# Half of a projection double chunk's closing sums added in device memory by accumulating DMAs

## The chip, the cores and the metric

The kernel runs on one core of a Trainium2 chip. The metric is the device time of one execution in microseconds (us); lower is better. Times before and after are medians of runs.

## The reference, cut to what matters

One layer works on 256 rows of 4096 channels, all in float32:

```
h    = layer_norm(x)                              # 256 x 4096
proj = h @ w_in                                   # 4096 x 24592
q_r,k_r,v_r,g_r, q_f,k_f,v_f,g_f, f, gate = split(proj)
y_r  = group_norm(retention(rotary(q_r), rotary(k_r), v_r)) * silu(g_r)
y_f  = forgetting_attention(q_f, k_f, v_f, f) * silu(g_f)
m    = sigmoid(gate0) * (y_r @ w_branch_ret) + sigmoid(gate1) * (y_f @ w_branch_fox)
out  = layer_norm(ALPHA * h + m @ w_out)
```

The first 16384 columns of `proj` (the eight operands of the two branches) are what the change touches. The kernel writes them to a device-memory scratch tensor, `proj_d`, and the branches read them back from there later.

## The kernel before, in words

A float32 product is made of three products of split operands: each operand is kept as a high part and a low part, and `three` (lines 198 to 200) multiplies high by high, high by low and low by high. The weights arrive as raw float32 in tiles `wraw` (three buffers, loaded by SP, line 137). `split_into` turns them into the two parts: ACT casts the high part (line 153) and the vector engine, DVE, subtracts it from the raw value (line 154).

The first part of the kernel makes the projection. After two gate chunks it works in double chunks of 1024 columns, 20 of them: four for gates and then 16 for the branches' operands. A double chunk goes over the 4096 input channels in 16 steps of 256 (`PAIRS`). In eight of these the 2 x 2 block product (two row tiles by two column halves) is made with eight block products, in the other eight (`SEVEN`) with seven, for which DVE forms sums of weight blocks (`ta`, `tb`, lines 184 to 187) and both engines split them (`tset`). TensorE, PE, so has 8 x 24 + 8 x 21 = 360 matmuls of 512 columns in a double chunk. They accumulate in all eight PSUM banks under the keys 1 to 7 and x: the plain steps add to 2, 3, 4 and x, which are the four output blocks, and the seven-product steps add to all but x.

At the end of a double chunk `proj_evac` has ACT copy the eight banks to SBUF tiles `ev` (line 397): two under the tag `bias`, six under `w1`. PE can't start the next double chunk's products in a bank before that copy. The closing sums are those of `combine` (line 402), a generator that `late_step` moves on by one piece after each step. For the branches' operands it runs eight DVE sums on `ev` tiles (line 416) and stores the four output blocks from GpSimd's queue (POOL, line 408, 256 KB each):

```
op("2", "2", "1", ALU.add)         # block (0,0) = 2 + 1
op("1", "6", "1", ALU.add)
op("5", "5", "1", ALU.add)
op("3", "3", "5", ALU.subtract)    # block (0,1) = 3 - (5 + 6 + 1)
op("1", "7", "1", ALU.add)
op("4", "4", "1", ALU.add)         # block (1,0) = 4 + (7 + 6 + 1)
op("5", "7", "5", ALU.add)
op("x", "x", "5", ALU.subtract)    # block (1,1) = x - (7 + 5 + 6 + 1)
```

The order on each engine isn't the order of the program: a planner simulates a timeline and issues what is ready there by priority, so the pieces of `combine` can stand close together behind the copies. A wait of an instruction holds up all that is queued behind it on its engine.

After the last double chunk the remaining gate chunks run, and beside them the generators `retention` and `forgetting`. These fetch their operands from `proj_d` on POOL's queue (line 466: `rab`, `v`, `gn`, `nat`). `silu` (line 476) takes the fetched `gn`. Then come the two branch projections and the output projection, which the change does not touch.

Of the kernel before, what the change touches and what calls it, by code (L numbers as in the profile page):

```python
# [10 lines left out]
AF = mybir.ActivationFunctionType  # L11
ALU = mybir.AluOpType

P = 128
# [9 lines left out]
NC = 512  # L24
# [11 lines left out]
def hybrid_kernel(  # L36
# [5 lines left out]
    nc = tc.nc  # L42
    x, b_gate, b_forget = aps["x"], aps["b_gate"], aps["b_forget"]
# [15 lines left out]
    proj_d = dram.tile([S, 4 * RW + 4 * FW], F32, name="proj_d")  # L59
# [4 lines left out]
    def bcast(ap1, n0, n):  # L64
        return ap1[n0:n0 + n].rearrange("(o n) -> o n", o=1).to_broadcast([P, n])
# [314 lines left out]
    late = []  # L380
# [8 lines left out]
    def proj_evac(c0, gate=False):  # L389
        def f(m):  # L390
            v = {}
            for i, k in enumerate("x1265374"):
                if i < 2:
                    v[k] = work.tile([P, NC], F32, name="ev", tag="bias", bufs=2)
                else:
                    v[k] = work.tile([P, NC], F32, name="ev", tag="w1", bufs=6)
                nc.scalar.copy(v[k], m[k])  # L397
            late.append(combine(c0, v, gate))
        return f

    def combine(c0, v, gate):


        def put(t, i, k):
            if gate:
                nc.scalar.activation(v[k], v[k], AF.Sigmoid)
            to = gates_d if gate else proj_d
            nc.gpsimd.dma_start(to[t * P:(t + 1) * P, c0 + i * NC:c0 + (i + 1) * NC], v[k])

        def shift(i):  # L410
            gb = work.tile([P, NC], F32, name="gshift", tag="gshift", bufs=1)
            nc.gpsimd.dma_start(gb, bcast(b_gate, c0 + i * NC, NC))
            return gb

        def op(o, x, y, how):
            nc.vector.tensor_tensor(v[o], v[x], v[y], op=how)

        yield
        if gate:
            gb = shift(0)  # L420
            yield
            yield
            nc.vector.tensor_tensor(v["1"], v["1"], gb, op=ALU.add)
            yield
            nc.vector.tensor_tensor(v["5"], v["5"], gb, op=ALU.subtract)
            gb = shift(1)
            yield
        op("2", "2", "1", ALU.add)
        put(0, 0, "2")
        yield  # L430
        op("1", "6", "1", ALU.add)
        yield
        if gate:
            nc.vector.tensor_tensor(v["5"], v["5"], gb, op=ALU.subtract)
            yield
        op("5", "5", "1", ALU.add)
        yield
        op("3", "3", "5", ALU.subtract)
        put(0, 1, "3")
        yield  # L440
        op("1", "7", "1", ALU.add)
        yield
        op("4", "4", "1", ALU.add)
        put(1, 0, "4")
        yield
        op("5", "7", "5", ALU.add)
        yield
        op("x", "x", "5", ALU.subtract)
        put(1, 1, "x")
# [435 lines left out]
    for i in range((GATE1 - GATE0) // 2):  # L885
        add_pair("w_in", hTh, hTl, sops, PAIRS, proj_evac(gates[GATE0 + 2 * i][0], True))
    for i in range(16):
        add_pair("w_in", hTh, hTl, sops, PAIRS, proj_evac(2 * i * NC))
# [239 lines left out]
```

## Time and profile before

| | before |
|---|---|
| median of 3 runs | 2848.55 us (2847.6 to 2850.07) |
| profiled execution | 2845.76 us |
| its span, first to last instruction | 2844.0 us |
| PE busy | 2793.1 us, 98% |
| DVE busy | 2305.3 us, 81% |
| ACT busy | 1565.1 us, 55% |
| POOL busy | 169.8 us, 6% |
| mean granted TensorE clock | 0.997 |

Busy time is the time in which an engine has an instruction in work; issuing DMAs does not count. A stall is the idle time just before an instruction, with the engine and line that released it. The profile counts its times from the span's start; the double chunks of the branches' operands run from about 453 to 1775 us.

### The profile page before, as it was taken

Reading aid. Unit: us, or ns where it says so; the run is one execution under the profiler, and the core shown is the slowest. Engines: PE = TensorE matmul, PEld = TensorE weight load, DVE = VectorE, ACT = ScalarE, POOL = GpSimd, SP = SyncE. Lnnn points to the kernel's source line nnn. Section 1 sums busy time; section 2 is a strip of 40 time slices with the busy share of each in tenths; the row PEclk is TensorE's granted clock in tenths of the full one; section 3 lists DMA queues with packets and bytes.
Section 4 is the critical chain, followed back from the end, with each engine's and each line's share of the span. In section 5 each row is a group of like instructions: output and inputs, shape, how many; then the busy total and the mean of one; then the engine's idle time right before and its main releaser. Section 6 shows DMA issues by size and latency. Waiting matters only on the chain. (4 is left out here: it accounts for less than half of the span.)

```text
span 2844.0 us, 34687 instructions
## 1 busy us (share of the span) xinstructions
PE 2793.1 (98%) x12666; PEld 2308.8 (81%) x12666; DVE 2305.3 (81%) x2988; ACT 1565.1 (55%) x2170; POOL 169.8 (6%) x302
## 2 busy tenths in 40 slices
PE   7999999999999999999999999999999999999998
PEld 5788888888887887888878888788898888888886
DVE  7899999998999988989889888877675656656666
ACT  5565666656555655555555565445664444444443
POOL 1000000000000000000000000212220000000000
PEclk9999999999999999999999999999999999999999
DMA  6556655665566655556656656866676566666564
GB/s 221 198 207 239 225 219 214 230 224 205 214 222 222 222 211 211 211 211 222 222 213 218 221 204 224 290 229 202 204 232 216 211 215 211 226 215 231 210 233 170
DMA packets 128156, 620.28 MB, mean 218 GB/s; under 512 B 15803, under 2 KB 16075, under 8 KB 87019
## 3 DMA queue, kind: packets, MB, share of 16 engines
q1 hardware_dynamic: 105552, 543.47, 52.8%
q0 software_dynamic: 21856, 72.49, 8.2%
q8 instruction: 99, 1.62, 0.2%
q10 hardware_dynamic: 576, 2.10, 0.2%
q14 instruction: 73, 0.60, 0.1%
HBM read 588.54 MB, written 29.46 MB: 217 GB/s over the span
## 5 line engine op out<-in xcount | busy, mean ns | idle before, releaser
L153 ACT CAST whi<-wraw 128x1024 fp32r<-128x1024 f32 (+1 forms) x640 | 586.3, 945 | 373.7 <-PE ps L200 262.1
L154 DVE TENSOR_TENSOR wpart<-wraw,wpart 128x512 fp32r<-128x512 f32 (+2 forms) x790 | 520.4, 667 | 314.0 <-ACT wpart L153 311.9
L153 ACT CAST wpart<-wraw 128x512 fp32r<-128x512 f32 (+2 forms) x790 | 475.3, 606 | 525.5 <-DVE wpart L154 314.4
L154 DVE TENSOR_TENSOR wlo<-wraw,whi 128x1024 fp32r<-128x1024 f32 (+1 forms) x640 | 680.8, 1084 | 8.7 <-ACT whi L153 7.2
L199 PE MATMUL ps<-wlo,hTh 128*128 128x512 f32 x960 | 373.7, 389 | 0.0
L200 PE MATMUL ps<-whi,hTl 128*128 128x512 f32 x960 | 373.4, 389 | 0.0
L198 PE MATMUL ps<-whi,hTh 128*128 128x512 f32 x960 | 340.2, 390 | 5.8 <-ACT ev L397 5.6
L184 DVE TENSOR_TENSOR ta<-wraw 128x1024 f32<-128x1024 f32 x160 | 195.6, 1222 | 137.6 <-DMA wraw<-in_w_in 136.5
L153 ACT CAST tset<-tb 128x1024 fp32r<-128x1024 f32 x160 | 169.3, 1058 | 183.8 <-DVE tb L187 183.6
L199 PE MATMUL acc<-wlo,hTh 128*128 128x512 f32 x640 | 249.1, 391 | 3.4 <-DVE wlo L154 3.4
L200 PE MATMUL acc<-whi,hTl 128*128 128x512 f32 x640 | 247.8, 389 | 0.0
L198 PE MATMUL acc<-whi,hTh 128*128 128x512 f32 x640 | 242.2, 389 | 0.4 <-ACT whi L153 0.4
L153 ACT CAST tset<-ta 128x1024 fp32r<-128x1024 f32 x160 | 167.6, 1048 | 120.1 <-DVE ta L184 119.8
L198 PEld LDWEIGHTS ps<-whi,hTh 128*128 128x128 f32 x960 | 180.2, 188 | 46.4 <-ACT ev L397 9.1
L199 PE MATMUL acc<-wpart,hTh 128*128 128x512 f32 (+2 forms) x568 | 212.2, 377 | 4.2 <-DVE wpart L154 4.1
L200 PEld LDWEIGHTS ps<-whi,hTl 128*128 128x128 f32 x960 | 180.2, 188 | 37.6
L199 PEld LDWEIGHTS ps<-wlo,hTh 128*128 128x128 f32 x960 | 180.2, 188 | 37.3
L200 PE MATMUL acc<-wpart,hTl 128*128 128x512 f32 (+2 forms) x568 | 208.2, 370 | 0.6 <-DVE rstd L96 0.6
L154 DVE TENSOR_TENSOR tset<-tb,tset 128x1024 fp32r<-128x1024 f32 x160 | 195.0, 1219 | 4.7 <-ACT tset L153 4.7
L154 DVE TENSOR_TENSOR tset<-ta,tset 128x1024 fp32r<-128x1024 f32 x160 | 194.8, 1217 | 0.4
L199 PE MATMUL acc<-wpart,mTh 128*128 128x512 f32 x500 | 194.6, 389 | 0.0
L200 PE MATMUL acc<-wpart,mTl 128*128 128x512 f32 x500 | 194.5, 389 | 0.0
(257 smaller groups left out, 4853.3 us busy)
## 6 DMA issues: line engine op xcount, KB each, us to landing
wraw<-in_w_in SPq DMA_DIRECT2D x320, 1024.0 KB, 4.9
wraw<-in_w_out SPq DMA_DIRECT2D x128, 512.0 KB, 4.1
wraw<-in_w_in SPq DMA_DIRECT2D x112, 512.0 KB, 4.8
wraw<-in_w_branch_ret SPq DMA_DIRECT2D x64, 512.0 KB, 4.2
wraw<-in_w_branch_fox SPq DMA_DIRECT2D x64, 512.0 KB, 4.2
proj_d<-ev POOLq DMA_DIRECT2D x64, 256.0 KB, 3.5
g<-gates_d POOLq DMA_DIRECT2D x16, 512.0 KB, 5.7
wraw<-in_w_in SPq DMA_DIRECT2D x16, 272.0 KB, 4.5
```

The source lines that it names most:

```text
L153: c = nc.scalar.copy(hi, src)
L154: nc.vector.tensor_tensor(lo, src, hi.bitcast(F32), op=ALU.subtract)
L184: nc.vector.tensor_tensor(ta, B[0][:, None, :].to_broadcast([P, 2, NC]), raw[:, NC:3 * NC].rearrange("p (a n) -> p a n", a=2), op=ALU.add)
L198: nc.tensor.matmul(o, lhsT=a[0], rhs=w[0], start=first, stop=False)
L199: nc.tensor.matmul(o, lhsT=a[0], rhs=w[1], start=False, stop=False)
L200: return nc.tensor.matmul(o, lhsT=a[1], rhs=w[0], start=False, stop=last)
```

## The change

The gate double chunks keep `combine`. For the other 16, `proj_evac` has ACT write the negative of bank 5, and a new generator, `gather`, stores the tiles 2, 3, 4 and x as they are, each to its output block in `proj_d`. DVE makes four sums on the other four tiles. Each result is then sent to one of the same blocks by a DMA that adds to what is there (`accum_op`). The accumulating DMA must wait until the plain store of its block has landed.

```diff
-                nc.scalar.copy(v[k], m[k])
-            late.append(combine(c0, v, gate))
+                if k == "5" and not gate:
+                    nc.scalar.activation(v[k], m[k], AF.Identity, scale=-1.0)
+                else:
+                    nc.scalar.copy(v[k], m[k])
+            late.append(combine(c0, v, True) if gate else gather(c0, v))
         return f
+
+    def gather(c0, v):
+
+
+        def put(t, i, k, how=None):
+            to = proj_d[t * P:(t + 1) * P, c0 + i * NC:c0 + (i + 1) * NC]
+            if how is None:
+                nc.gpsimd.dma_start(to, v[k])
+            else:
+                nc.gpsimd.dma_start(to, v[k], accum_op=how)
+
+        def op(o, x, y, how):
+            nc.vector.tensor_tensor(v[o], v[x], v[y], op=how)
+
+        yield
+        for t, i, k in ((0, 0, "2"), (0, 1, "3"), (1, 0, "4"), (1, 1, "x")):
+            put(t, i, k)
+            yield
+        put(0, 0, "1", ALU.add)
+        op("6", "6", "1", ALU.add)
+        yield
+        op("5", "5", "6", ALU.subtract)
+        put(0, 1, "5", ALU.add)
+        yield
+        op("6", "6", "7", ALU.add)
+        put(1, 0, "6", ALU.add)
+        yield
+        op("7", "5", "7", ALU.subtract)
+        put(1, 1, "7", ALU.add)
```

## Rows read from the trace of the kernel before

**Rows 1.** The page's first part: busy us (share), instructions.
```profile
PE 2793.1 (98%) x12666; PEld 2308.8 (81%) x12666; DVE 2305.3 (81%) x2988; ACT 1565.1 (55%) x2170; POOL 169.8 (6%) x302
```
**Rows 2.** PE's waits, 480 to 1800 us: waiter, releaser, total us, times, longest.
```profile
PE ps L198 <- ACT ev L397: 4.4, 6, 1.4
PE acc L199 <- DVE wlo L154: 3.4, 4, 1.0
PE acc L199 <- DVE wpart L154: 2.1, 1, 2.1
PE acc L198 <- ACT tset L153: 0.9, 2, 0.4
PE acc L198 <- ACT whi L153: 0.4, 1, 0.4
```
**Rows 3.** PE's timeline, rows with a stall: start, us, what, idle before.
```profile
1042.41 0.50 PE L199 MATMUL acc<-wlo,hTh 128*128 128x512 f32 x1 [1.00 <-DVE wlo L154]
...
1704.41 0.50 PE L199 MATMUL acc<-wlo,hTh 128*128 128x512 f32 x1 [0.41 <-DVE wlo L154]
1706.15 0.50 PE L199 MATMUL acc<-wlo,hTh 128*128 128x512 f32 x1 [1.00 <-DVE wlo L154]
```
**Rows 4.** DVE's timeline behind the double chunk's end at about 1030 us.
```profile
1029.85 0.68 DVE L416 TENSOR_TENSOR ev<-ev 128x512 f32<-128x512 f32 x1
...
1040.54 0.68 DVE L416 TENSOR_TENSOR ev<-ev 128x512 f32<-128x512 f32 x1
1041.14 1.22 DVE L154 TENSOR_TENSOR wlo<-wraw,whi 128x1024 fp32r<-128x1024 f32 x1
```
**Rows 5.** Groups by line and shape: busy us, mean ns of one, idle before.
```profile
L416 DVE TENSOR_TENSOR ev<-ev 128x512 f32<-128x512 f32 x160 | 106.7, 683 | 0.0
L397 ACT COPY ev<-ps 128x512 f32<-128x512 f32 x80 | 47.9, 620 | 0.0
L406 ACT ACTIVATE ev<-ev 128x512 f32<-128x512 f32 x16 | 10.3, 645 | 1.9 <-DVE ev L416 1.9
L634 ACT ACT_TABLE_LOAD x5 | 6.4, 1283 | 0.4 <-DVE nm L631 0.3
```
**Rows 6.** Windows: length, busy PE, PEld, DVE, ACT, POOL, clock, DMA share, GB/s.
```profile
1442.00:1470.00 28.00, 26.58 (x114) 20.85 (x113) 27.52 (x33) 18.20 (x24) 2.16 (x4) 1.00 0.63 230
1470.00:1524.00 54.00, 54.00 (x240) 44.71 (x239) 46.13 (x50) 30.02 (x32) 0.00 (x0) 1.00 0.57 206
1780.00:1800.00 20.00, 17.81 (x86) 14.28 (x85) 17.50 (x25) 9.24 (x15) 7.25 (x12) 1.00 0.99 367
```
**Rows 7.** DMA, 1442 to 1470 us: POOL's queue; issues, median us to landing.
```profile
q0 software_dynamic: 320, 1.05, 9.4%
wraw<-in_w_in SPq DMA_DIRECT2D x5, 1024.0 KB, 6.3
proj_d<-ev POOLq DMA_DIRECT2D x4, 256.0 KB, 3.7
```
**Rows 8.** The same view, 1470 to 1524 us.
```profile
wraw<-in_w_in SPq DMA_DIRECT2D x11, 1024.0 KB, 4.8
```
**Rows 9.** POOL's timeline where the branches begin.
```profile
1774.96 1.45 POOL L466 DMA_DIRECT2D rab<-proj_d  x2 [8.14 <-PE ps L200]
1776.91 0.57 POOL L408 DMA_DIRECT2D proj_d<-ev  x1 [0.49 <-DVE ev L416]
...
1783.05 0.73 POOL L466 DMA_DIRECT2D gn<-proj_d  x1
```
**Rows 10.** Line 408 alone: its DMAs' time to landing, all of the span.
```profile
DMA to landing us min/median/max: 2.3/3.7/8.8
```
**Rows 11.** ACT's timeline and PE's, just behind.
```profile
1791.56 1.06 ACT L476 ACTIVATE sg<-gn 128x1024 f32<-128x1024 f32 x1 [0.48 <-DMA gn<-proj_d]
1789.22 0.50 PE L199 MATMUL acc<-wpart,hTh 128*128 128x512 f32 x1 [2.10 <-DVE wpart L154]
```

## The prediction

> **What bounds the kernel now.** I read the page's busy times first [rows 1]: PE is busy 98% of the span, so whatever is done on another engine can only win back PE's idle time. The second view is the list of what PE waited for between 480 and 1800 us, the stage of the changed sums and the hand-over to the branches [rows 2]. The reader should see how short it is: 4.4 + 3.4 + 2.1 + 0.9 + 0.4 = 11.2 us in 1320. That is the ceiling for named gains, 0.39% of the time. The three kinds have different causes. Six stalls wait for ACT to empty a PSUM bank at a double chunk's end (4.4 us). Seven wait for a split weight on DVE or ACT (3.4 + 0.9 + 0.4 = 4.7 us). One, of 2.1 us, comes at 1789 us, where the branches begin.
>
> The third view is PE's timeline, which says where the seven lie: all follow a double chunk's end by 12 to 14 us, and only five of the 16 ends have any; the first and the last end's are shown [rows 3]. DVE's timeline there gives the reason [rows 4]: the eight closing sums stand from 1029.85 to 1040.54 between the splits, the late split starts at 1041.14, and PE starts at 1042.41. The windows say the same in shares [rows 6]: in the 28 us around an end DVE is busy 27.52 us, in the 54 us behind it 46.13. So DVE has slack in a double chunk but none around its end, and that is where the change acts.
>
> **What the change removes.** Four of eight sums go, in 16 double chunks: 64 sums. One shows as 683 ns [rows 5], but the next DVE instruction starts 0.60 us after it (1040.54 to 1041.14, rows 4), so an end loses 4 x 0.60 = 2.4 us of DVE's queue and the whole stage 38 us. Of these, only what PE waits for counts. At the worst end the two stalls make 0.41 + 1.00 = 1.41 us [rows 3]; no other of the seven is over 1.0 [rows 2]. All are shorter than 2.4, so with loads on time all 4.7 us go. The bounds are 0 (the planner puts other work in the freed slots) and -4.7.
>
> **What it adds on ACT.** The negated copy of bank 5 is an activation in place of a copy. The trace has no such instruction on a bank; the nearest row is the sigmoid of the same size, 645 ns against 620 for a copy [rows 5]. I take 25 ns longer: 16 x 0.025 = 0.4 us of ACT, with PE's bank 5 behind it at most, so nothing to 0.4 on the path. Bounds: a little less than a copy, or, were the tables to be loaded each time, 1.28 us [rows 5] x 16 = 20.5 us of ACT, half of which could reach PE. I take 0, since ACT is idle a third of the 28 us (18.20 busy, rows 6).
>
> **What it adds on the DMA engines.** Instead of four stores an end has eight DMAs of 256 KB, four of them accumulating. What a plain one takes follows from POOL's queue around an end [rows 7]: four take 9.4% of 28 us, 2.6 us or 0.66 us each of all 16 engines. No row shows an accumulating one. From below it is 0.66 us, since as many bytes leave SBUF; from above I take the whole 3.7 us that a plain store needs to land [rows 7], as if the engines were held all that time. The DMA engines are idle for 37% of the 28 us [rows 6], 10.4 us, so between 2.6 and 14.8 us are wanted where 10.4 are free. I take 0.66, the measured row nearest to it.
>
> Free on average is not free for each load. Weight loads take 6.3 us around an end [rows 7] and 4.8 behind it [rows 8]. I put the 1.5 us between down to the four stores, and let four more cost another 1.5. A load that comes later makes DVE later by as much, so of the 2.4 us won 0.9 are left. The two ends with one stall of 1.00 keep 0.1 each (3.4 less the 1.41 of the last end leaves 2.0 for two), the last keeps 0.5, the rest go: 4.7 - 0.7 = 4.0 us gained. That is the first term.
>
> **Queues and waits.** POOL issues the four stores as soon as ACT has copied 2, 3, 4 and x, and doesn't wait for DVE any more. Behind them the first accumulating DMA waits for its store to land, 3.7 us [rows 7], by which time ACT is just through its copies; the other three wait for DVE's sums. In the projection only other DMAs of `gather` are queued behind. The `ev` tiles are held until the last accumulating DMA has landed, two landings of 3.7 us and four sums behind the copies, and are wanted again only at the next end, some 82 us on (16 ends between 453 and 1775 us). SP's queue and the loads' order don't move.
>
> At the hand-over it is different. POOL's queue holds the branches' fetches among the last stores [rows 9], and the DMA engines are busy 99% from 1780 to 1800 us [rows 6]. There the DVE relief of 2.4 us covers the stall of 2.1 [rows 11], but 4 x 0.66 = 2.6 us more of DMA come out of a full machine: -2.1 + 2.6 = +0.5 us, the second term.
>
> **Sum.** -4.0 + 0.5 = -3.5 us. The profiled execution took 2845.76 us (span 2844.0 and 1.8 around it), which gives 2842.3; it is 2.8 us below the median of the runs, 2848.55, and on that scale I predict 2845.0.
>
> **Rivals.**
> *An accumulating DMA costs like two plain ones.* It has to fetch what lies in the block before it writes, so twice the bytes move. Then the four cost 5.3 us, the loads are not 1.5 but 3.0 us later, and this is 0.6 more than DVE wins. The five ends that already stall get 5 x 0.6 = 3.0 us worse, and the hand-over is -2.1 + 5.3 = +3.2. Together +6.2 if every delay reaches PE, some +3.5 if half the hand-over's and two thirds of the ends' do: 2852. For it: the bytes. Against: 10.4 us of idle DMA around an end, and 11 ends that have slack. The row shows 0.66 us for a plain store [rows 7]. The Trainium skill ("Collectives: The Full Stack", section "The bandwidth ceiling: the fold count and why AG ≠ RS ≠ AR") says that an add inside a DMA costs nothing itself but needs two source reads, and so gives half a copy's rate; by it the price would be an estimated 1.3 us and the time this rival's, by the row alone it is the forecast's. No run here has shown it yet.
>
> *POOL's queue is held at the hand-over.* If the planner puts the first accumulating DMA before the fetch of `gn`, that fetch waits until a store has landed. Issued at 1776.9 and landing in up to 8.8 us [rows 10], the store frees the queue at 1785.7, so `gn` goes 2.7 us later than at 1783.05 [rows 9]. ACT's sigmoid already waits for it, 0.48 us [rows 11], and the weight casts are queued behind. That is +2.7 on the forecast: 2847.7. Against: the planner may fetch first.
>
> *The banks' stalls go as well.* With less on DVE the splits that ACT does before its copies come earlier, and the 4.4 us [rows 2] fall too, with the hand-over's 2.1: -11.2, 2837.3. For: the copies wait in ACT's order behind casts. Against: those casts depend on work from before the closing sums, which the change doesn't touch.
>
> *Slower: the accumulating DMAs hold the engines.* At 3.7 us each, 14.8 us are wanted in a 28 us window with 10.4 free. The loads lose 4.4 us at every end, DVE has gained 2.4, so PE loses 2.0 x 16 = 32 us, and 14.8 - 2.1 = 12.7 at the hand-over: +45, 2893. It decides from (10.4 + 2.4) / 4 = 3.2 us each. For: nothing in the trace accumulates, so nothing rules it out. Against: three times what even doubled bytes would ask.
>
> **How the numbers follow.** Forecast 0.40; doubled cost 0.20; POOL held 0.10; banks too 0.15; engines held 0.15. A measurement can't tell under 0.2%, 5.7 us, from no change. Faster by more (below 2842.8) is the banks' case and a tenth of the forecast's and others' spread: 0.24. Slower by more (above 2854.3) is the held engines and a third of the doubled cost: 0.22. The same: 0.54. The range goes from the banks' case, 2838, to 2862, a held-engines case that is just past its deciding point; it leaves out most of that case and a little below.
>
> **What would show it.** Line 416 should have 96 sums in place of 160 and DVE some 40 us less busy time. The seven stalls 12 us behind an end should be nearly gone, the bank stalls stay near 4.4 us. Weight loads around an end should land in about 7.8 us, accumulating DMAs in no more than 5, and DMA share should be 0.72 instead of 0.63. At the hand-over PE's stall should stay near 2 to 3 us. I am wrong if an accumulating DMA takes well over 1.3 us of the engines, if PE stalls appear at ends that had none, or if the bank stalls change by more than 3 us.

## The result, and the profile after

The changed kernel takes 2890.34 us (median of 4 runs, 2886.89 to 2893.39) against 2848.07 for the one before on the same chip: 42 us more, ratio 1.0151 with a 95% interval of 1.0131 to 1.017. Slower was clear, and outside my range. The profiled execution took 2892.81 us, 47.1 more than that of before.

The page's first part and POOL's DMA queue of the changed kernel (busy us and share; packets, MB, share of 16 engines):

```profile
PE 2812.1 (97%) x12666; PEld 2311.9 (80%) x12666; DVE 2271.4 (79%) x2924; ACT 1561.2 (54%) x2170; POOL 227.9 (8%) x366
...
q0 software_dynamic: 31072, 89.27, 11.3%
```

DVE did lose its 64 sums (2988 to 2924 instructions) and 34 us of busy time [rows 1]. POOL's busy time does count its DMA issues: the 64 accumulating ones are nearly all of the 58 us that it gained. What PE waited for between 480 and 1800 us:

```profile
PE ps L198 <- ACT ev L400: 15.6, 8, 3.0
PE acc L198 <- ACT tset L153: 11.9, 12, 2.2
PE acc L199 <- DVE wlo L154: 5.7, 7, 1.1
PE acc L199 <- DVE tset L154: 2.4, 6, 0.4
PE acc L198 <- ACT whi L153: 0.9, 2, 0.7
```

The 11.2 us of [rows 2] have become 36.5. The wait for ACT's copies at an end, 4.4 before, is the largest, and 18 stalls in place of two wait for `tset`. These stalls don't show all: adding up by how much the starts of successive matmuls lie further apart than their usual 0.227 us, from 540 to 1770 us, PE lost 17 us before and 62 after. So the whole loss is in the projection.

A double chunk's end of the changed kernel and the calm stretch behind it, then 4 us of the first (columns as in [rows 6]):

```profile
1389.00:1417.00 28.00, 25.74 (x107) 20.97 (x106) 24.94 (x28) 18.25 (x24) 5.71 (x8) 0.94 0.82 261
1417.00:1471.00 54.00, 54.00 (x240) 44.72 (x240) 46.18 (x48) 29.91 (x32) 0.00 (x0) 1.00 0.58 209
1392.00:1396.00 4.00, 4.00 (x12) 3.11 (x12) 3.91 (x6) 4.00 (x8) 1.88 (x4) 0.57 0.71 199
```

Around this end the DMA engines are busy 82% of the time (63% before) and DVE 24.94 of 28 us (27.52 before): DVE has got its slack, and PE has lost more. The last row shows a side effect: behind a stall of 2.26 us the granted clock was 0.57 for 4 us, mostly the lower of TensorE's two levels (1.2 and 2.4 GHz). That came at three ends, 5 us in all.

The DMA view of those 28 us, to be read against [rows 7]:

```profile
q0 software_dynamic: 896, 2.10, 31.2%
...
wraw<-in_w_in SPq DMA_DIRECT2D x5, 1024.0 KB, 6.6
proj_d<-ev POOLq DMA_DIRECT2D x8, 256.0 KB, 6.0
```

POOL's DMAs take 31.2% of 28 us, 8.7 us, where the four plain stores took 2.6. Over 14 ends the mean is 8.9 us, so an accumulating DMA costs (8.9 - 2.6) / 4 = 1.57 us of all 16 engines against 0.66 for a plain one, 2.4 times. The Trainium skill ("Collectives: The Full Stack", section "The bandwidth ceiling: the fold count and why AG ≠ RS ≠ AR") has a collective's adding transfers at half a copy's rate because the add needs two source reads; the trace agrees in kind, at somewhat more than double, and doesn't show what is read.

POOL's timeline at the same end, and line 412 (the accumulating DMAs) by its own view and its group beside the negated copy (line 398) and the sums (line 415):

```profile
1391.74 0.57 POOL L410 DMA_DIRECT2D proj_d<-ev  x1 [69.02 <-ACT ev L400]
1392.72 0.56 POOL L410 DMA_DIRECT2D proj_d<-ev  x1 [0.40 <-ACT ev L400]
1394.69 0.54 POOL L410 DMA_DIRECT2D proj_d<-ev  x1 [1.41 <-ACT ev L400]
1395.54 0.88 POOL L412 DMA_DIRECT2D proj_d<-ev  x1 [0.31 <-DMA proj_d<-ev]
1397.55 0.56 POOL L410 DMA_DIRECT2D proj_d<-ev  x1 [1.13 <-ACT ev L400]
1400.54 1.75 POOL L412 DMA_DIRECT2D proj_d<-ev  x2 [2.43 <-DMA proj_d<-ev]
1405.11 0.85 POOL L412 DMA_DIRECT2D proj_d<-ev  x1 [2.82 <-DMA proj_d<-ev]
```
```profile
DMA to landing us min/median/max: 4.7/8.2/13.0
```
```profile
L412 POOL DMA_DIRECT2D proj_d<-ev x64 | 56.5, 938 | 107.3 <-DMA proj_d<-ev 90.4 <-DVE ta L184 8.2 <-DVE ev L415 3.6
L415 DVE TENSOR_TENSOR ev<-ev 128x512 f32<-128x512 f32 x64 | 44.0, 688 | 1.9
...
L398 ACT ACTIVATE ev<-acc 128x512 f32<-128x512 f32 x16 | 10.0, 622 | 0.0
```

All eight DMAs go out within 14 us of the end, and the accumulating ones take a median of 8.2 us to land.

### The profile page after: what moved, and what is told of

The parts are those of the page before. It is cut to its first block, busy times and chain, and to the rows that moved or that the text cites. A ratio compares the mean times of both kernels' runs of the same rounds, so it can differ in the third digit from the quotient of the medians.

```text
span 2891.0 us, 34731 instructions
## 1 busy us (share of the span) xinstructions
PE 2812.1 (97%) x12666; PEld 2311.9 (80%) x12666; DVE 2271.4 (79%) x2924; ACT 1561.2 (54%) x2170; POOL 227.9 (8%) x366
## 5 line engine op out<-in xcount | busy, mean ns | idle before, releaser
L153 ACT CAST whi<-wraw 128x1024 fp32r<-128x1024 f32 (+1 forms) x640 | 583.0, 944 | 294.7 <-PE ps L200 204.2
L184 DVE TENSOR_TENSOR ta<-wraw 128x1024 f32<-128x1024 f32 x160 | 196.0, 1225 | 210.9 <-DMA wraw<-in_w_in 210.6
L198 PE MATMUL ps<-whi,hTh 128*128 128x512 f32 x960 | 332.7, 391 | 16.2 <-ACT ev L400 16.1
```

The costliest lines, as they stand in the source:

```text
L153: c = nc.scalar.copy(hi, src)
L184: nc.vector.tensor_tensor(ta, B[0][:, None, :].to_broadcast([P, 2, NC]), raw[:, NC:3 * NC].rearrange("p (a n) -> p a n", a=2), op=ALU.add)
L198: nc.tensor.matmul(o, lhsT=a[0], rhs=w[0], start=first, stop=False)
```

## The experiments

Each ran beside the kernel before on one chip; differences are to its median there (2846 to 2848 us). "Engine time" is POOL's DMA time, the queue's share times the length of the window, a mean over 14 or 15 ends; "landing" is that of the weight loads, the median of an end's, in the same way, within 26 us of an end.

```
kernel            extra DMAs of an end        engine time, us     landing  time
                                              0-26     26-66      us       us
before            -                           2.6      0          5.6      -
changed           4 accumulating, early       8.8      0.1        7.4      +42.3
e1_plain          4 plain, early              5.3      0          6.5      +18.8
e2_drop           none, 4 sums only           2.7      0          5.4       0.0
e3_narrow         4 accumulating, 1/8 wide    4.7      0          5.6      +6.2
e4_before_acc     4 accumulating, 8 sums      7.1      2.8        6.3      +37.0
e5_late           4 accumulating, late        2.7      6.4        5.6      +26.2
e8_late_plain     4 plain, late               2.7      2.5        5.6      -2.8
e9_late_three     12 plain, late              2.7      7.4        5.6      +29.3
e10_lone          3 accumulating, late        2.0      5.4        5.4      +17.9
e6_spread         none, sums + stores late    0.7      2.0        5.1      -12.9
e11_spread_gates  as e6, gates' sums too      0.7      2.0        5.1       -5.4
e12_late_stores   none, stores late           0        2.6        4.9      -4.9
```

Behind 66 us another 1.0 us falls in e5_late, 0.9 in e9_late_three and 0.3 in e8_late_plain. The landing column doesn't see the late DMAs: in the 40 us behind the first 26, a load takes a mean of 5.0 us before, 5.2 in e8_late_plain, 5.7 in e5_late, 5.9 in e9_late_three and 6.1 in e10_lone.

**The same order, plain stores (e1_plain).**

```diff
-                nc.gpsimd.dma_start(to, v[k], accum_op=how)
+                nc.gpsimd.dma_start(to, v[k])
```

> The changed kernel with its four accumulating DMAs of an end turned into plain stores to the same blocks, with the same waits and the same order of instructions on every engine. It overwrites blocks in place of adding. Theory A (an accumulating DMA takes the DMA engines about 1.5 us where a plain one takes 0.66, and this makes the weight loads late): most of the 44 us go, 2846 to 2862. Theory B (the planner's new order of the splits, copies and matmuls is what PE waits for): the time stays within 8 us of the changed kernel's, 2882 to 2898. Theory C (it is the burst of eight DMAs at an end, whatever their kind): 2865 to 2890.

2864.87 us (2861.81 to 2869.04), ratio 1.0073 [1.0056, 1.009]. Every engine has the changed kernel's order, so 23.5 of the 42.3 us are what accumulating costs over a store. The other 18.8 come with four more plain stores of 0.66 us, in the new order. It lies a little above theory A's range and at the edge of C's: both have a share. Theory B, the order alone, is out.

**No second half (e2_drop), and a narrow one (e3_narrow).** The first leaves out the accumulating DMAs, so the blocks hold half of their sums; the second adds only 64 of 512 columns.

```diff
-                nc.gpsimd.dma_start(to, v[k], accum_op=how)
+                pass                                                                          # e2_drop
+                nc.gpsimd.dma_start(to[:, 0:64], v[k][:, 0:64], accum_op=how)                 # e3_narrow
```

> The changed kernel without its four accumulating DMAs of an end (the second half of each block's sum never arrives); the four DVE sums stay. The planner's order changes a little. Theory A and C: no extra DMA is left and DVE has 2.4 us less to do at an end, so the time falls to before or just below, 2840 to 2849, and the stalls of before 12 us behind an end are gone. Theory B: 2865 to 2895.

> The changed kernel with the accumulating DMAs cut to 64 of 512 columns: as many rows, an eighth of the bytes (the other columns lack their second half). If the price of an accumulating DMA goes with its bytes, four take some 0.8 us of the engines in place of 6 and the time is 2842 to 2852. If it goes with its rows or is fixed for each DMA, they take over 4 us and the time is 2865 to 2890. Theory B: 2875 or more either way.

e2_drop: 2846.09 us, ratio 0.9996 [0.9987, 1.0006]: as before. PE's waits from 480 to 1800 us:

```profile
PE acc L199 <- DVE tset L154: 1.5, 4, 0.6
PE ps L493 <- DVE rry L539: 0.5, 1, 0.5
PE ps L198 <- ACT ev L400: 0.3, 2, 0.2
PE acc L199 <- DVE wlo L154: 0.2, 1, 0.2
```

The stalls of 11.2 us fall to 2.5, as theory A has it, and PE's lost time from 17 to 12 us; but the median of ten runs shows nothing of it. The saving on DVE is worth at most 3.7 us here (the interval's end). This run also sends its four stores earlier, 1 to 7 us behind ACT's first copy in place of 4 to 17, and what that costs isn't separated from the saving. e3_narrow: 2852.35 us, 1.0023 [1.0011, 1.0034]. Its accumulating DMAs take (4.7 - 2.6) / 4 = 0.51 us each, a third of a full one's for an eighth of its bytes; 2852.35 is just past the upper end for a price by bytes, and neither pure form holds. Nor is engine time the whole price: its 2.1 us more cost 6 us and leave the landing at 5.6, where the 2.7 us more of e1_plain cost 19 and make it 6.5. No run shows why.

**The traffic without the saving (e4_before_acc).** Each stored tile is added once more to its block, which comes out doubled.

```diff
             nc.gpsimd.dma_start(to[t * P:(t + 1) * P, c0 + i * NC:c0 + (i + 1) * NC], v[k])
+            if not gate:
+                nc.gpsimd.dma_start(to[t * P:(t + 1) * P, c0 + i * NC:c0 + (i + 1) * NC], v[k], accum_op=ALU.add)
```

> The kernel before, all eight DVE sums kept, with an accumulating DMA of the same tile to the same block behind each of the four stores (so each block comes out doubled). It has the change's DMA traffic and none of its saving on DVE. Theory A and C: as slow as the changed kernel or slower, 2885 to 2915. Theory B: near before, 2846 to 2860.

2883.07 us, 1.013 [1.0115, 1.0145], 2 us below the range of A. Up to the branches every engine but POOL has the order of the kernel before, so 37 us of loss come with the DMAs alone. With all eight sums kept the loss is even 5 us smaller than the changed kernel's. That doesn't show the four saved sums to be worthless: the DMAs here wait for the sums, and 2.8 of their 9.9 us fall later than 26 us.

**Out of the end's 28 us (e5_late, e8_late_plain).** `last[0]` is DVE's latest split when the piece is issued; the planner may not put the sum ahead of it. The two have one order on every engine. Cut to the loop's body; the last double chunk stays as before.

```diff
+            with tc.issue_after(last[0]):
+                op(o, a, y, how)
+            if t is not None:
+                acc = put(t, i, o, ALU.add)          # e8_late_plain: a plain store
+                if o == "5":
+                    with tc.issue_after(acc):
+                        put(0, 0, "1", ALU.add)
+            yield
+            yield
```

> The changed kernel with the four DVE sums, and so the accumulating DMAs that wait for them, held back until DVE has done later splits: one sum about every 10 us, from some 20 us behind an end on; the first block's accumulating DMA goes behind the second's. The last double chunk sums on DVE as before. As many accumulating DMAs (60 for 64), the same 1.57 us each. Theory A1 (extra DMA time makes PE wait because it falls into the 28 us around an end, where DVE has no slack and the loads come late; one such DMA at a time in the calm 54 us is covered by slack): 2846 to 2858. Theory A2 (the loads have no slack anywhere, each extra us of DMA time delays PE by a share of it wherever it stands): 2872 to 2892.

> As the run with the late accumulating DMAs, in the same order on every engine, but with plain stores in their place (blocks are overwritten, not added to): 0.66 us of the DMA engines each in place of 1.57. Theory A1: 2844 to 2852, within 6 us of its accumulating twin, where the early pair differed by 25. Theory A2: 2858 to 2870, some 20 us below the twin.

e5_late: 2872.87 us, 1.009 [1.0075, 1.0106]. e8_late_plain: 2843.95 us, 0.9994 [0.9982, 1.0005]. Neither theory holds by itself. Four plain stores cost 18.8 us early and, together with four late sums, nothing late, as A1 said; but accumulating ones still cost 29 us more than their plain twins, as A2 said. Counted through to the next end, 2.8 us of late DMA time in a double chunk went without a net loss and 7.3 did not. That the 2.8 are free by themselves isn't shown: late sums are a gain of their own, as e6_spread below suggests, and four late sums without extra stores were not run.

One place in e5_late, to show where the loss comes up: POOL's issues, the DMA engines just behind them (share 1.01 of ten us, at 266 GB/s), and PE at the next end:

```profile
738.18 1.78 POOL L414 DMA_DIRECT2D proj_d<-ev  x2 [29.81 <-DVE ev L417]
747.40 0.84 POOL L414 DMA_DIRECT2D proj_d<-ev  x1 [7.44 <-DVE ev L417]
```
```profile
740.00:750.00 10.00, 10.00 (x46) 8.29 (x45) 7.75 (x10) 4.31 (x5) 0.84 (x1) 1.00 1.01 266
```
```profile
785.25 0.50 PE L200 MATMUL ps<-whi,hTh 128*128 128x512 f32 x1 [1.05 <-ACT ev L402]
```

PE doesn't stop in those ten us. It stops 40 us later, where ACT has to copy the banks behind a cast that came late. Of e5_late's 20 us of stalls 9 are at the copies. That this stall goes back to those DMAs is argued from the order of events; the plain twin has no stall at this end.

**Engine time or kind (e9_late_three), and one at a time (e10_lone).** The first makes three plain stores of each late DMA, two of them to spare tensors; the second sums the first block on DVE and spaces the other three.

```diff
-    proj_d = dram.tile([S, 4 * RW + 4 * FW], F32, name="proj_d")
+    proj_d, spare0, spare1 = (dram.tile([S, 4 * RW + 4 * FW], F32, name=n_) for n_ in ("proj_d", "spare0", "spare1"))
...
+                return [nc.gpsimd.dma_start(d[t * P:(t + 1) * P, c0 + i * NC:c0 + (i + 1) * NC], v[k]) for d in (spare0, spare1, proj_d)][2].ins
```
```diff
+        with tc.issue_after(last[0]):
+            op("2", "2", "1", ALU.add)
+        put(0, 0, "2")
```

> The late kernel with each accumulating DMA turned into three plain stores of the same tile, two of them to spare tensors that nobody reads (blocks are overwritten, not added to). Three take 3 x 0.68 = 2.0 us of the DMA engines, a little more than one accumulating DMA's 1.6 to 1.8. If it is the engines' time that delays the loads and then PE, this kernel is as slow as its accumulating twin, 2865 to 2885. If an accumulating DMA hurts by its kind (what it does to the loads beside it), more stores of the plain kind stay near the plain twin, 2842 to 2855.

> The late kernel with the first block summed on DVE (five DVE sums, three accumulating DMAs) and a piece more between them, so that none stands beside another; the late kernel issues its first two back to back. If the price falls on each accumulating DMA alike (26 us for 60), 45 cost 20: 2864 to 2870. If it is the pair that makes a load so late that PE waits and a single one is covered, 2844 to 2852.

e9_late_three: 2875.93 us, 1.0098 [1.0083, 1.0113]. Twelve late plain stores an end take 8.4 us of the engines through to the next end, where the four accumulating DMAs take 7.3, and cost 29 us against 26: plain stores of as much engine time do as much harm, so the adding by itself isn't needed for it. The planner's order differs a little between the two. Its bank stalls alone are 19.4 us:

```profile
PE ps L200 <- ACT ev L402: 19.4, 14, 2.6
```

e10_lone: 2864.55 us, 1.0063 [1.0049, 1.0077]: 45 lone ones cost 18 us, as many each (0.40 us) as the 60 of e5_late (0.44). Pairs are not needed for the loss.

**What the freed place is worth (e6_spread, e11_spread_gates, e12_late_stores).** No accumulating DMA: the first holds the eight sums, and so the stores behind them, back as in e5_late; the second does so in the gate double chunks too; the third leaves the sums at the end and holds only the stores.

```diff
+        spread = not gate and c0 < 15 * 2 * NC            # e11_spread_gates: gate or c0 < ...
...
         def op(o, x, y, how):
-            nc.vector.tensor_tensor(v[o], v[x], v[y], op=how)
+            if spread:
+                with tc.issue_after(last[0]):
+                    nc.vector.tensor_tensor(v[o], v[x], v[y], op=how)
...
```
```diff
+                p_ = nc.gpsimd.tensor_copy(tick, ...)     # two columns of a later split
+                with tc.issue_after(p_.ins):
+                    put(t, i, k)
```

> The kernel before with its eight DVE sums spread over the double chunk: each is held behind the split that DVE did last when its piece was issued, from two steps later on, with no accumulating DMA and no extra store (the last double chunk stays as before). If PE's stalls 12 us behind an end (4.7 us) are due to the eight sums standing close together, they go, and the time is 2840 to 2844. If they only move to other places, 2845 to 2848. If the sums now meet splits that have no slack either, over 2849.

> The spread kernel (eight DVE sums held behind later splits, no accumulating DMA) with the four gate double chunks spread in the same way. Their three ends before 453 us show few stalls, so: 2831 to 2835, no clear difference from the spread kernel's 2833.8; if the gate ends had hidden lateness too, 2826 to 2831; if the shift rows held in a single buffer now come late, over 2836.

> The kernel before with its eight DVE sums left close behind an end, and only the four stores held back: each waits, on POOL, for a copy of two columns of a later split, so that one store goes out about every 10 us from some 25 us behind an end on. No accumulating DMA. The spread kernel (sums and stores both late) took 12.6 us off. If that came from the stores leaving the 28 us around an end, this one takes 2833 to 2839; if it came from the sums, 2844 to 2849; if it needs both, between.

e6_spread: 2833.76 us (2831.53 to 2836.91), 0.9956 [0.9944, 0.9969], 13 us better than before and the fastest of all, beyond the range I gave. Its POOL issues behind one end, and PE's waits from 480 to 1800 us:

```profile
1042.83 0.54 POOL L410 DMA_DIRECT2D proj_d<-ev  x1 [46.16 <-DVE ev L422]
1059.64 0.55 POOL L410 DMA_DIRECT2D proj_d<-ev  x1 [16.27 <-DVE ev L422]
1072.45 0.54 POOL L410 DMA_DIRECT2D proj_d<-ev  x1 [12.26 <-DVE ev L422]
1082.20 0.54 POOL L410 DMA_DIRECT2D proj_d<-ev  x1 [9.22 <-DVE ev L422]
```
```profile
PE ps L200 <- ACT ev L399: 3.5, 3, 2.2
PE acc L201 <- DVE wpart L154: 1.0, 1, 1.0
```

The same eight sums and four stores, a store every 10 to 17 us, leave 4.5 us of stalls. e12_late_stores: 2842.03 us, 0.9983 [0.9974, 0.9992], so the stores' place alone gives 5 of the 13 us, and the other 8 need the sums' place too. e11_spread_gates: 2841.24 us, 0.9984 [0.9975, 0.9993], 7 us worse than without the gates. Why is open: by the spacing of the matmuls PE loses 16 us up to 540 us in both profiles, so the gates' ends don't show it.

## Why the prediction was wrong

**The ceiling and the saving.** PE's 11.2 us said nothing of how much can be lost, and they were no ceiling for gains either: e6_spread won 13 us, since PE loses more time than its named stalls (17 us by the spacing of its matmuls). Fewer sums did what I said to the stalls (e2_drop: the waits fall to 2.5 us), but the 4.0 us I booked for it don't show in the median: 0.0, at most 3.7, with the earlier stores in it.

**ACT.** 622 ns against 595 for a copy of the same kind of bank: 27 ns, 25 forecast, and no table load.

**The price of an accumulating DMA.** I took the lower bound, 0.66 us; it is 1.57. The bounds, 0.66 and 3.7, held. The rival with the doubled price had the price nearly right and still gave 2852, because it let the delays reach PE by the same rule.

**The step that failed: "let four more cost another 1.5. A load that comes later makes DVE later by as much, so of the 2.4 us won 0.9 are left."** The landing I gave was nearly right, by luck: the loads around an end land 1.8 us later each (5.6 to 7.4), but four plain stores, which is what I had priced, add 0.9 (6.5 in e1_plain), and the accumulating DMAs are dearer than that. Wrong was to count the delay once for an end, against 2.4 us of relief, and to let only the five ends pay that stalled already. By that rule a delay under 2.4 us costs nothing new. e1_plain has one of 0.9 us and lost 18.8, the changed kernel one of 1.8 and lost 42. PE lost 45 us more over some 15 double chunks, 3 us in each, mostly where my sum had booked no loss: 15.6 us at the next ends' copies, which I had said would stay at 4.4, and 13.5 us from 24 us behind an end on, where before had no stall. All three signs of being wrong that I had named came. One such place in the changed kernel, 30 us behind an end, DVE and then PE:

```profile
1073.78 1.23 DVE L184 TENSOR_TENSOR ta<-wraw 128x1024 f32<-128x1024 f32 x1 [4.33 <-DMA wraw<-in_w_in]
```
```profile
1076.14 0.50 PE L198 MATMUL acc<-tset,soh 128*128 128x512 f32 x1 [1.53 <-ACT tset L153]
```

**Why the idle DMA engines were no cover.** I read 37% idle as 10.4 us free. SP's own waits, 535 to 1770 us, before and after, show what that idle time is:

```profile
SPq L137 <- DVE wlo L154: 988.8, 207, 9.2
SPq L137 <- DVE tb L187: 155.9, 33, 10.7
```
```profile
SPq L137 <- DVE wlo L154: 1055.9, 207, 12.5
SPq L137 <- DVE tb L187: 69.6, 22, 3.7
```

In both kernels SP stands for nine tenths of the time before a buffer that DVE has not freed (1145 and 1126 of 1235 us): a load isn't asked for until then. The engines idle because nothing has been requested, and when a load runs, DVE will soon wait for it. A DMA beside it is then not in a gap but in the loop load, split, free, load. A load that lands late frees its buffer late. Two groups of the page, before and after, show the lead of the splits over PE shrink:

```profile
L184 DVE TENSOR_TENSOR ta<-wraw 128x1024 f32<-128x1024 f32 x160 | 195.6, 1222 | 137.6 <-DMA wraw<-in_w_in 136.5
L153 ACT CAST whi<-wraw 128x1024 fp32r<-128x1024 f32 (+1 forms) x640 | 586.3, 945 | 373.7 <-PE ps L200 262.1
```
```profile
L184 DVE TENSOR_TENSOR ta<-wraw 128x1024 f32<-128x1024 f32 x160 | 196.0, 1225 | 210.9 <-DMA wraw<-in_w_in 210.6
L153 ACT CAST whi<-wraw 128x1024 fp32r<-128x1024 f32 (+1 forms) x640 | 583.0, 944 | 294.7 <-PE ps L200 204.2
```

DVE waits 210.6 us for loads in place of 136.5. ACT waits for PE to free a split's buffer, which it does where the splits are ahead, 204.2 us in place of 262.1. One instruction takes as long as before (1222 and 1225 ns, 945 and 944), so the DMAs didn't slow DVE or ACT at their work. That this loop adds up the delays is read from these waits and from the table, not tried by itself: a fourth buffer would have been the test, and no run has one.

**The hand-over.** +0.5 forecast. In the 80 us behind the last end's copies PE's stalls are 0.24, 1.00, 0.97 and 0.17 us, where they were 2.10 and 0.63. POOL's queue waited for landing stores and the sigmoid for `gn` 1.72 us (0.48 before), but PE's stalls didn't grow.

**The slow rival.** "Engines held" named 2893, and the kernel took 2890, but by another way: it asked for 3.7 us each and let nothing happen below 3.2. At 1.57, half of that, the whole loss was there, since its deciding point came from the same idle share. That its time came out near the measured one is chance.

## What to carry to other kernels

An idle share of the DMA engines need not be room for other transfers, as it was not here. Where each load waits for a buffer that its predecessor frees, price an added transfer as delay in that loop, and look for its cost at the next tight place, not beside it. Before work is moved from an engine to the DMA engines because it is in the way at one place, move it to another place on its own engine: here moving the sums and their stores gave 13 us (5 of them the stores' place), and the DMA version lost 42.

## What the runs showed of the hardware

- An accumulating DMA of 256 KB from SBUF to device memory took 1.57 us of all 16 engines and 8.2 us to land at an end, against 0.66 and 6.0 for a plain one in its place (e1_plain). In the calm stretch it took 1.8 and 5.4 (e5_late), against 0.7 and 3.8 (e8_late_plain). One of 32 KB with as many rows took 0.51 (e3_narrow).
- POOL needed 938 ns to issue an accumulating DMA and 588 for a plain one.
